# Scales of four token tiles at once, and squares of the mixer outputs summed on TensorE, in a hybrid attention and state-space layer

## The chip, the cores and the metric

One core of a Trainium2 chip runs the whole program. The metric is device time in microseconds (us), and lower is better. The kernel is written on a layer that takes tiles from pools, orders the instructions of each engine in a planner that simulates time, and then puts in the semaphore waits by itself. Each engine works through its own queue in that order.

## The reference

One decoder layer over 1024 tokens of width 1024. What matters here:

```python
mod = silu(c) @ ada_w + ada_b                    # sh1, sc1, g1, sh2, sc2, g2
h = modulate(rmsnorm(x, norm1_g), sh1, sc1)
p = h @ w_in                                     # q, k, v (512 each), u (512)
q = rmsnorm(q.reshape(L, 8, 64), q_norm_g)       # per token and head
k = rmsnorm(k.reshape(L, 8, 64), k_norm_g)
o_attn = stick_breaking(q, k, v)                 # strictly causal, 8 heads
o_ssm = s5(u, ...)                               # 32 groups of 16 channels
o = concat(rmsnorm(o_attn, attn_out_g), rmsnorm(o_ssm, ssm_out_g))
x = x + g1 * (o @ w_out)
h = modulate(rmsnorm(x, norm2_g), sh2, sc2)
x = x + g2 * ((gelu(gate) * val) @ ffn_w_down)   # val, gate: causal conv of h @ ffn_w_up
```

## The kernel before, in words

The program is one straight sequence without loops at run time. Its stages in the profiled execution are: norm and projection of u (0 to 95 us); projections of q, k and v, with the four batches of the state-space part and most of the modulation vectors among them (95 to 342 us); attention over eight heads, with the output projection of the state-space half as filler (342 to 580 us); the output projection of the attention half and the second norm (565 to 660 us); the gated MLP (to the end).

The middle stage is what the change touches first. Two loops (L592 to L625) run over q and k (cix) and over pairs of token tiles (tq). For each of the two tiles j of a pair, `proj` (L549) makes 24 products into a PSUM tile (tag "mm", three of them); ScalarE copies it to the SBUF tile `qk` (L603) and squares it in place (L605); VectorE sums the squares by head into `qssq` (L606). Then, once for a pair, VectorE forms 1/sqrt in 12 small operations on 16 columns (L607, and `rsqrt`, L71 to L80: a shift, a seed, three Newton rounds of three operations). Then both tiles are scaled (L611), transposed on TensorE (L615), split into a high and a low part `hl` (L618 to L622), and written to DRAM (L624).

In front of every projection stands `ada_step(3)` (L601): three steps of a generator (`ada_back`, L560) that makes the modulation vectors g1, sh2 and sc2. For each of six blocks `ix` it takes one tile `ada_acc` [128, 512], clears it on GpSimd, and then eight times loads a tile `ada_raw` of 256 KB through SyncE's DMA queue (L568) and adds it, times one column, to `ada_acc` on VectorE (L569, recorded as L67). At the end of a block TensorE sums over partitions (`adps`, L573 or L577). `ada_acc`, `ada_raw` and the tile `uF` of `u_evac` (L197) share one tag "uF" with three buffers in the pool `wp`. While a block runs, `ada_acc` holds one of the three, so two are left for `ada_raw`. What is left of the generator after the last projection of v runs at L649. 48 loads and 48 VectorE operations are made in all.

Then the pools `psA`, `stg`, `wp` and `hp` are released (L653 to L656), and the attention's pools `op_`, `wo`, `osp`, `psZ`, `psT`, `psM`, `ap_` take their memory (L657 to L662). All pools are made with `reuse_waits="tile"` (L58).

`mix_scale` (L750) gives the scale of the norm of the mixer outputs. For each token tile ScalarE squares four slices of 128 channels into `osq` (L755; one buffer), VectorE adds the four slices into `otot` (L757), and one product with a column of ones sums over partitions into a column of `nps` (L758). It runs for eight token tiles of the state-space half early in the attention (`ssm_stats`, L789), and for eight tiles of the attention half in the last head (`tail_stats`, L837).

Of the kernel before, what the change touches and what calls it, by code (L numbers as in the profile page):

```python
# [9 lines left out]
F32 = mybir.dt.float32  # L10
# [3 lines left out]
AF = mybir.ActivationFunctionType  # L14
ALU = mybir.AluOpType
AX = mybir.AxisListType
# [19 lines left out]
def hybrid_layer_kernel(  # L36
# [17 lines left out]
    act, dve, pool, pe, sp = nc.scalar, nc.vector, nc.gpsimd, nc.tensor, nc.sync  # L54
# [5 lines left out]
    def tt(eng, out, a, b, op):  # L60
        eng.tensor_tensor(out=out, in0=a, in1=b, op=op)  # L61
# [7 lines left out]
    MUL, ADD, SUB = ALU.mult, ALU.add, ALU.subtract  # L69

    def rsqrt(pl, dst, v, n):  # L71

        i = pl.tile([128, n], I32, tag="rs_i", name="rs_i")
        h = pl.tile([128, n], F32, tag="rs_h", name="rs_h")
        dve.tensor_scalar(out=i, in0=v.bitcast(I32), scalar1=1, scalar2=None, op0=ALU.logical_shift_right)
        ts(dve, dst.bitcast(I32), i, -1.0, RSQRT_SEED, MUL, ADD)
        for _ in range(3):
            stt(h, dst, -0.5, dst, MUL, MUL)
            tt(dve, h, h, v, MUL)
            stt(dst, h, 1.5, dst, ADD, MUL)  # L80
# [3 lines left out]
    small = alloc("small", bufs=2)  # L84
# [13 lines left out]
    ones = const.tile([128, 128], F32, name="ones")  # L98
# [34 lines left out]
    wp = alloc("w_in")  # L133
# [60 lines left out]
            pe.matmul(o, lhsT=ll, rhs=rh, start=False, stop=(k == 7))  # L194

    def u_evac(m, hf):
        uF = wp.tile([128, 8, 64], F32, tag="uF", name="uF", bufs=3)  # L197
        act.activation(out=uF, in_=u_ps[m, hf].rearrange("p (c j) -> p j c", j=8), func=AF.Copy)
        sp.dma_start(out=u_d[m * 128:(m + 1) * 128, :, hf * 64:(hf + 1) * 64], in_=uF)

# [348 lines left out]
    def proj(cix, t, his, los):  # L549
        o = psA.tile([128, 512], F32, tag="mm", name="qkvp", bufs=3)  # L550
        for k in range(NK):
            lh, ll = hhi[k][:, t * 128:(t + 1) * 128], hlo[k][:, t * 128:(t + 1) * 128]
            pe.matmul(o, lhsT=lh, rhs=his[k], start=(k == 0), stop=False)  # L553
            pe.matmul(o, lhsT=lh, rhs=los[k], start=False, stop=False)  # L554
            pe.matmul(o, lhsT=ll, rhs=his[k], start=False, stop=(k == NK - 1))  # L555
        return o
# [3 lines left out]
    def ada_back(ix):  # L560

        kind, o = divmod(ix * 512, 1024)
        acc = wp.tile([128, 512], F32, tag="uF", name="ada_acc", bufs=3)
        pool.memset(acc, 0.0)
        sp.dma_start(out=acc[0:1, :], in_=ada_br[ix:ix + 1, :])
        for r in range(8):
            raw = wp.tile([128, 512], F32, tag="uF", name="ada_raw", bufs=3)
            sp.dma_start(out=raw, in_=ada_r[ix, :, r])  # L568
            stt(acc, raw, c_sb[:, r:r + 1], acc, MUL, ADD)  # L569
            yield  # L570
        ps = psA.tile([128, 512], F32, tag="aux", name="adps")
        if kind == 0:
            pe.matmul(ps, lhsT=ones, rhs=acc, start=True, stop=True)  # L573
            act.activation(out=g1row[:, o:o + 512], in_=ps, func=AF.Copy)
        else:
            for j in range(4):
                pe.matmul(ps[:, j:j + 1], lhsT=acc[:, j * 128:(j + 1) * 128], rhs=ones[:, 0:1], start=True, stop=True)  # L577
            ks = slice(o // 128, o // 128 + 4)
            if kind == 1:
                act.activation(out=S2c[:, ks], in_=ps[:, 0:4], func=AF.Copy)  # L580
            else:
                stt(A2[:, ks], ps[:, 0:4], 1.0, n2g_sb[:, ks], ADD, MUL)
        yield
# [7 lines left out]
    ssm_at = {(0, 0): 0, (0, 1): 1, (0, 3): 2, (1, 1): 3}  # L591
    for cix in range(2):  # L592
        his, los = load_wchunk(cix)
        for tq in range(4):
            if (cix, tq) in ssm_at:
                ssm_batch(ssm_at[cix, tq])
            qk = stg.tile([128, 2, 8, 64], F32, tag="qk", name="qk", bufs=2)
            ssq = small.tile([128, 2, 8], F32, tag="qssq", name="qssq")
            inv = small.tile([128, 2, 8], F32, tag="qinv", name="qinv")
            for j in range(2):  # L600
                ada_step(3)  # L601
                o = proj(cix, tq * 2 + j, his, los)
                act.activation(out=qk[:, j].rearrange("p h d -> p (h d)"), in_=o, func=AF.Copy)  # L603
                ov = o.rearrange("p (h d) -> p h d", d=64)
                act.activation(out=o, in_=o, func=AF.Square)  # L605
                dve.tensor_reduce(out=ssq[:, j, :], in_=ov, op=ADD, axis=AX.X)  # L606
            ts(dve, ssq, ssq, 1.0 / HD, EPS, MUL, ADD)  # L607
            rsqrt(small, inv.rearrange("p a b -> p (a b)"), ssq.rearrange("p a b -> p (a b)"), 16)
            for j in range(2):
                t = tq * 2 + j  # L610
                tt(dve, qk[:, j], qk[:, j], inv[:, j, :].unsqueeze(2).to_broadcast([128, 8, 64]), MUL)  # L611
                tp = psA.tile([128, 512], F32, tag="qt", name="qkT", bufs=1)
                qf = qk[:, j].rearrange("p h d -> p (h d)")
                for a_ in range(4):
                    pe.transpose(tp[:, a_ * 128:(a_ + 1) * 128], qf[:, a_ * 128:(a_ + 1) * 128], ident)  # L615
                hl = stg.tile([128, 2, 512], F32R, tag="hl", name="hl", bufs=2)
                if cix == 0:
                    act.activation(out=hl[:, 0], in_=tp, func=AF.Copy, scale=gqk)  # L618
                    stt(hl[:, 1], tp, gqk, hl[:, 0].bitcast(F32), MUL, SUB)
                else:  # L620
                    act_copy(hl[:, 0], tp)
                    tt(dve, hl[:, 1], tp, hl[:, 0].bitcast(F32), SUB)  # L622
                for r in range(2):
                    act.dma_start(out=qk_d[cix, r].rearrange("(a p) t -> p a t", p=128)[:, :, t * 128:(t + 1) * 128],  # L624
                                 in_=hl[:, r].bitcast(F32).rearrange("p (a t) -> p a t", t=128))  # L625
# [124 lines left out]
    def mix_scale(pl, ps, src, ts_, jc, inv):  # L750

        for c, t in enumerate(ts_):
            s_, v = mix_view(src, t, jc)
            sq = pl.tile([128, 4, 128], F32, tag="osq", name="osq", bufs=1)
            act.activation(out=v(sq), in_=s_, func=AF.Square)  # L755
            tot = pl.tile([128, 128], F32, tag="otot", name="otot", bufs=1)
            dve.tensor_reduce(out=tot, in_=sq.rearrange("p k c -> p c k"), op=ADD, axis=AX.X)  # L757
            pe.matmul(ps[:, c:c + 1], lhsT=tot, rhs=ones[:, 0:1], start=True, stop=True)  # L758
            yield
        n = len(ts_)  # L760
        ssq = small.tile([128, n], F32, tag="ossq", name="ossq")
        ts(dve, ssq, ps[:, 0:n], 1.0 / 512.0, EPS, MUL, ADD)
        rsqrt(small, inv, ssq, n)
# [506 lines left out]
```

## Time and profile before

| | us |
|---|---|
| median of 3 runs | 1331.42 (1327.92 to 1335.95) |
| profiled execution | 1326.97 |
| its span | 1324.6 |
| PE busy | 1213.3 (92%) |
| DVE busy | 1010.3 (76%) |
| ACT busy | 587.1 (44%) |
| POOL busy | 467.5 (35%) |

The span runs from the first to the last instruction of the profiled execution; 2.4 us lie around it. PE is TensorE, DVE VectorE, ACT ScalarE, POOL GpSimd, SP SyncE; SPq is the queue through which SyncE issues transfers. A busy share over the whole span is a mean over stages with different limits, so the stages are read one by one.

### The profile page before, as it was taken

Reading aid. Unit: us, or ns where it says so; the run is one execution under the profiler, and the core shown is the slowest. Engines: PE = TensorE matmul, PEld = TensorE weight load, DVE = VectorE, ACT = ScalarE, POOL = GpSimd, SP = SyncE. Lnnn points to the kernel's source line nnn. Section 1 sums busy time; section 2 is a strip of 40 time slices with the busy share of each in tenths; the row PEclk is TensorE's granted clock in tenths of the full one; section 3 lists DMA queues with packets and bytes.
Section 4 is the critical chain, followed back from the end, with each engine's and each line's share of the span. In section 5 each row is a group of like instructions: output and inputs, shape, how many; then the busy total and the mean of one; then the engine's idle time right before and its main releaser. Section 6 shows DMA issues by size and latency. Waiting matters only on the chain.

```text
span 1324.6 us, 16659 instructions
## 1 busy us (share of the span) xinstructions
PE 1213.3 (92%) x5752; PEld 992.6 (75%) x5752; DVE 1010.3 (76%) x1543; ACT 587.1 (44%) x1003; POOL 467.5 (35%) x367
## 2 busy tenths in 40 slices
PE   5879899989678989679999998999999999999998
PEld 4767778767566777567777876788888888888887
DVE  6999997983788898988898878878887773345334
ACT  5431233331475677546654534454545453223220
POOL 4462443430563344930035544345554510000000
PEclk9898889999778999789999999999999999999999
DMA  8462455558943666115022233222222165447442
GB/s 342 163 144 50 117 139 152 143 140 231 265 105 96 204 188 203 42 56 170 30 88 103 81 104 104 96 96 72 96 72 96 49 203 186 143 160 253 148 138 104
DMA packets 125631, 177.83 MB, mean 134 GB/s; under 512 B 36454, under 2 KB 73958, under 8 KB 124524
## 3 DMA queue, kind: packets, MB, share of 16 engines
q1 hardware_dynamic: 105484, 156.85, 38.0%
q10 hardware_dynamic: 20064, 19.93, 4.5%
q8 instruction: 45, 0.74, 0.2%
q14 instruction: 38, 0.31, 0.1%
HBM read 134.67 MB, written 40.89 MB: 133 GB/s over the span
## 4 chain that ended last, share of the span: by engine, by line
PE 58%; DVE 25%; DMA 7%; issue 5%; ACT 3%; POOL 2%; SPq 1%; DVEq 0%; ACTq 0%; POOLq 0%
PE dnps L1181 6%; PE dnps L1180 6%; PE dnps L1182 6%; PE up_a L986 5%; PE up_a L985 5%; PE up_a L987 5%; DVE ada_acc L67 3%; DMA ada_raw<-in_ada_r_dram 3%; DVE nb L703 3%; PE up_c L986 2%; PE up_c L987 2%; PE up_c L985 2%; PE wops L776 2%; DVE cv L67 2%; PE wops L778 2%
## 5 line engine op out<-in xcount | busy, mean ns | idle before, releaser
L67 DVE SCALAR_TENSOR_TENSOR cv<-up,cols_sb,cv 128x1023 f32<-128x1023 f32 (+1 forms) x88 | 136.6, 1554 | 16.6 <-ACT cv L1106 15.9
L61 POOL TENSOR_TENSOR S<-upraw 128x512 f32<-128x512 f32 x40 | 72.8, 1820 | 208.0 <-DMA upraw<-in_w_up_dram 144.7
L61 DVE TENSOR_TENSOR alo<-araw,ahi 128x1024 fp32r<-128x1024 f32 x44 | 53.9, 1224 | 120.2 <-ACT ahi L160 120.1
L1181 PE MATMUL dnps<-wdlo,ahi 128*128 128x512 f32 x352 | 136.9, 389 | 0.0
L1182 PE MATMUL dnps<-wdhi,alo 128*128 128x512 f32 x352 | 136.9, 389 | 0.0
L1180 PE MATMUL dnps<-wdhi,ahi 128*128 128x512 f32 x352 | 134.7, 389 | 0.0
L61 POOL TENSOR_TENSOR sig<-sig,nb 128x127 f32<-128x127 f32 (+3 forms) x64 | 93.2, 1464 | 84.4 <-DVE nb L703 53.7
L160 ACT ACTIVATE ahi<-araw 128x1024 fp32r<-128x1024 f32 x44 | 46.6, 1059 | 144.4 <-PE dnps L1181 127.3
L703 DVE TENSOR_TENSOR_SCAN nb<-nb 128x128 f32<-128x128 f32 (+3 forms) x64 | 108.6, 1710 | 1.5 <-ACT nb L701 1.2
L61 DVE TENSOR_TENSOR uplo<-S,uphi 128x512 fp32r<-128x512 f32 x80 | 90.7, 1140 | 19.8 <-ACT uphi L160 19.4
L67 DVE SCALAR_TENSOR_TENSOR ada_acc<-ada_raw,c_sb,ada_acc 128x256 f32<-128x256 f32 (+1 forms) x97 | 75.0, 787 | 24.9 <-DMA ada_raw<-in_ada_r_dram 23.0
L160 ACT ACTIVATE uphi<-S 128x512 fp32r<-128x512 f32 x80 | 49.1, 625 | 89.5 <-POOL S L61 69.4
L61 POOL TENSOR_TENSOR cv<-cv 128x1024 f32<-128x1024 f32 x22 | 53.9, 2451 | 98.3 <-ACT cv L1110 88.8
L553 PE MATMUL qkvp<-w_hi,hhi 128*128 128x512 f32 x192 | 78.3, 409 | 5.6 <-DVE qssq L606 2.9
L554 PE MATMUL qkvp<-w_lo,hhi 128*128 128x512 f32 x192 | 78.1, 407 | 0.8 <-POOL w_lo L61 0.8
L555 PE MATMUL qkvp<-w_hi,hlo 128*128 128x512 f32 x192 | 78.2, 407 | 0.0
L1180 PEld LDWEIGHTS dnps<-wdhi,ahi 128*128 128x128 f32 x352 | 66.1, 188 | 13.8
L1182 PEld LDWEIGHTS dnps<-wdhi,alo 128*128 128x128 f32 x352 | 66.1, 188 | 13.7
L1181 PEld LDWEIGHTS dnps<-wdlo,ahi 128*128 128x128 f32 x352 | 66.1, 188 | 13.6
L160 ACT ACTIVATE uphi<-upraw 128x512 fp32r<-128x512 f32 x68 | 41.7, 627 | 55.8 <-PE up_c L986 22.4
L710 PE MATMUL wT<-ident,sig 128*128 128x128 f32 x288 | 50.4, 302 | 14.1 <-POOL sig L61 8.7
L714 ACT ACTIVATE wh<-wT 128x512 fp32r<-128x512 f32 (+2 forms) x96 | 45.4, 497 | 37.6 <-PE wT L710 24.2
(328 smaller groups left out, 3479.5 us busy)
## 6 DMA issues: line engine op xcount, KB each, us to landing
upraw<-in_w_up_dram SPq DMA_DIRECT2D x88, 256.0 KB, 3.1
araw<-a_d SPq DMA_DIRECT2D x44, 512.0 KB, 3.5
ada_raw<-in_ada_r_dram SPq DMA_DIRECT2D x48, 256.0 KB, 3.0
a_d<-cv ACTq DMA_DIRECT2D x22, 512.0 KB, 2.6
wdraw<-in_w_down_dram SPq DMA_DIRECT2D x44, 256.0 KB, 3.6
ada_raw<-in_ada_a_dram SPq DMA_DIRECT2D x8, 1024.0 KB, 9.4
qk_d<-hl ACTq DMA_DIRECT2D x32, 256.0 KB, 2.9
q<-qk_d SPq DMA_DIRECT2D x32, 256.0 KB, 5.7
```

The costliest lines, as they stand in the source:

```text
L61: eng.tensor_tensor(out=out, in0=a, in1=b, op=op)
L67: dve.scalar_tensor_tensor(out=out, in0=a, scalar=s, in1=b, op0=op0, op1=op1)
L160: act.activation(out=o, in_=i, func=AF.Copy)
L553: pe.matmul(o, lhsT=lh, rhs=his[k], start=(k == 0), stop=False)
L555: pe.matmul(o, lhsT=ll, rhs=his[k], start=False, stop=(k == NK - 1))
L703: dve.tensor_tensor_scan(out=nb[:, 0:n][:, ::-1], data0=nb[:, 0:n][:, ::-1], data1=nb[:, 0:n][:, ::-1], initial=1.0, op0=MUL, op1=ALU.bypass)
L985: pe.matmul(ps, lhsT=hi[:, kt, :], rhs=rh, start=(first and kt == 0), stop=False, skip_group_check=True)
L986: pe.matmul(ps, lhsT=hi[:, kt, :], rhs=rl, start=False, stop=False, skip_group_check=True)
L987: pe.matmul(ps, lhsT=lo[:, kt, :], rhs=rh, start=False, stop=(kt == 3), skip_group_check=True)
L1180: pe.matmul(o[t], lhsT=hi[:, a], rhs=whi, start=(m == 0), stop=False)
L1181: pe.matmul(o[t], lhsT=hi[:, a], rhs=wlo, start=False, stop=False)
L1182: pe.matmul(o[t], lhsT=lo[:, a], rhs=whi, start=False, stop=(m == NM - 1))
```

## The change

Three things are done.

The loop over pairs becomes a loop over groups of four tiles: `qssq` and `inv` have 32 columns, the 12 small operations run once for four tiles, and scaling and transposes of four tiles follow. The tiles `qk` become single ones with five buffers (before: double ones with two). The batches of the state-space part keep their places between the projections.

The tag "uF" goes from three buffers to two, for `uF`, `ada_acc` and `ada_raw` alike.

In `mix_scale` the addition on VectorE and the tile `otot` are gone; four products, one for each slice of `osq`, accumulate in the column of `nps`. `osq` gets two buffers.

```diff
     def u_evac(m, hf):
-        uF = wp.tile([128, 8, 64], F32, tag="uF", name="uF", bufs=3)
+        uF = wp.tile([128, 8, 64], F32, tag="uF", name="uF", bufs=2)
...
-        acc = wp.tile([128, 512], F32, tag="uF", name="ada_acc", bufs=3)
+        acc = wp.tile([128, 512], F32, tag="uF", name="ada_acc", bufs=2)
...
-            raw = wp.tile([128, 512], F32, tag="uF", name="ada_raw", bufs=3)
+            raw = wp.tile([128, 512], F32, tag="uF", name="ada_raw", bufs=2)
...
-        for tq in range(4):
-            if (cix, tq) in ssm_at:
-                ssm_batch(ssm_at[cix, tq])
-            qk = stg.tile([128, 2, 8, 64], F32, tag="qk", name="qk", bufs=2)
-            ssq = small.tile([128, 2, 8], F32, tag="qssq", name="qssq")
-            inv = small.tile([128, 2, 8], F32, tag="qinv", name="qinv")
-            for j in range(2):
+        for tq in range(2):
+            qks = []
+            ssq = stg.tile([128, 4, 8], F32, tag="qssq", name="qssq")
+            inv = stg.tile([128, 4, 8], F32, tag="qinv", name="qinv")
+            for j in range(4):
+                if (cix, tq * 2 + j / 2) in ssm_at:
+                    ssm_batch(ssm_at[cix, tq * 2 + j // 2])
                 ada_step(3)
-                o = proj(cix, tq * 2 + j, his, los)
-                act.activation(out=qk[:, j].rearrange("p h d -> p (h d)"), in_=o, func=AF.Copy)
+                o = proj(cix, tq * 4 + j, his, los)
+                qk = stg.tile([128, 8, 64], F32, tag="qk", name="qk", bufs=5)
+                qks.append(qk)
+                act.activation(out=qk.rearrange("p h d -> p (h d)"), in_=o, func=AF.Copy)
...
-            rsqrt(small, inv.rearrange("p a b -> p (a b)"), ssq.rearrange("p a b -> p (a b)"), 16)
-            for j in range(2):
-                t = tq * 2 + j
-                tt(dve, qk[:, j], qk[:, j], inv[:, j, :].unsqueeze(2).to_broadcast([128, 8, 64]), MUL)
+            rsqrt(stg, inv.rearrange("p a b -> p (a b)"), ssq.rearrange("p a b -> p (a b)"), 32)
+            for j in range(4):
+                t = tq * 4 + j
+                tt(dve, qks[j], qks[j], inv[:, j, :].unsqueeze(2).to_broadcast([128, 8, 64]), MUL)
...
-            sq = pl.tile([128, 4, 128], F32, tag="osq", name="osq", bufs=1)
+            sq = pl.tile([128, 4, 128], F32, tag="osq", name="osq", bufs=2)
             act.activation(out=v(sq), in_=s_, func=AF.Square)
-            tot = pl.tile([128, 128], F32, tag="otot", name="otot", bufs=1)
-            dve.tensor_reduce(out=tot, in_=sq.rearrange("p k c -> p c k"), op=ADD, axis=AX.X)
-            pe.matmul(ps[:, c:c + 1], lhsT=tot, rhs=ones[:, 0:1], start=True, stop=True)
+            for kk in range(4):
+                pe.matmul(ps[:, c:c + 1], lhsT=sq[:, kk, :], rhs=ones[:, 0:1], start=(kk == 0), stop=(kk == 3))
```

## Rows read from the trace of the kernel before

**Rows 1.** Busy time by engine, with share of the span and instructions (page, part 1).

```profile
PE 1213.3 (92%) x5752; PEld 992.6 (75%) x5752; DVE 1010.3 (76%) x1543; ACT 587.1 (44%) x1003; POOL 467.5 (35%) x367
```

**Rows 2.** Busy time by stretch: stretch, length, engines (instructions), clock, DMA share, GB/s.

```profile
95.00:190.00 95.00, 82.78 (x425) 68.21 (x425) 91.36 (x197) 22.21 (x36) 33.89 (x30) 0.88 0.40 102
...
292.00:342.00 50.00, 43.43 (x210) 35.74 (x210) 19.53 (x29) 9.33 (x16) 3.98 (x8) 0.98 0.70 208
342.00:420.00 78.00, 59.04 (x286) 46.63 (x285) 69.23 (x82) 50.13 (x108) 48.84 (x44) 0.73 0.56 151
...
565.00:640.00 75.00, 66.52 (x321) 54.41 (x321) 61.54 (x167) 41.70 (x82) 9.41 (x10) 0.95 0.33 113
```

**Rows 3.** The chain that ended last, at 292 us: start, duration, what.

```profile
292.50 3.12 DMA ada_raw<-in_ada_r_dram
295.72 0.76 DVE ada_acc L67
296.50 3.66 DMA ada_raw<-in_ada_r_dram
```

**Rows 4.** Waits of SyncE's queue, 60 to 345 us: total us, times, longest.

```profile
SPq L568 <- DVE ada_acc L67: 53.1, 30, 6.2
```

**Rows 5.** Timeline of DVE: start, duration, line, operation, releaser of idle time before.

```profile
122.42 0.74 DVE L67 SCALAR_TENSOR_TENSOR ada_acc<-ada_raw,c_sb,ada_acc 128x512 f32<-128x512 f32 x1
...
139.23 0.75 DVE L67 SCALAR_TENSOR_TENSOR ada_acc<-ada_raw,c_sb,ada_acc 128x512 f32<-128x512 f32 x1
...
291.72 0.75 DVE L67 SCALAR_TENSOR_TENSOR ada_acc<-ada_raw,c_sb,ada_acc 128x512 f32<-128x512 f32 x1
...
338.83 0.75 DVE L67 SCALAR_TENSOR_TENSOR ada_acc<-ada_raw,c_sb,ada_acc 128x512 f32<-128x512 f32 x1 [2.11 <-DMA ada_raw<-in_ada_r_dram]
```

**Rows 6.** Timeline of PE where the projections end and attention begins.

```profile
335.47 0.39 PE L555 MATMUL qkvp<-w_hi,hlo 128*128 128x512 f32 x1
339.69 1.35 PE L577 MATMUL adps<-ones,ada_acc 128*128 128x1 f32 x8 [3.83 <-issue]
340.90 0.45 PE L697 MATMUL z<-k,q 128*128 128x128 f32 x1
```

**Rows 7.** The small DVE operations of L607 and L608, 95 to 345 us, by form.

```profile
L67 DVE SCALAR_TENSOR_TENSOR rs_h<-qinv 128x16 f32<-128x16 f32 x24 | 9.5, 402 | 0.2
...
L75 DVE TENSOR_SCALAR rs_i<-qssq 128x16 int32<-128x16 int32 x8 | 6.3, 787 | 0.0
...
L61 DVE TENSOR_TENSOR rs_h<-rs_h,qssq 128x16 f32<-128x16 f32 x24 | 5.7, 243 | 0.2
...
L67 DVE SCALAR_TENSOR_TENSOR qinv<-rs_h,qinv 128x16 f32<-128x16 f32 x24 | 5.0, 215 | 0.3
L64 DVE TENSOR_SCALAR qinv<-rs_i 128x16 int32<-128x16 int32 x8 | 4.3, 538 | 0.0
L64 DVE TENSOR_SCALAR qssq<-qssq 128x16 f32<-128x16 f32 x8 | 2.8, 350 | 0.1
```

**Rows 8.** The addition in `mix_scale`, products with one column, and PE's wait (360 to 420 us).

```profile
L757 DVE TENSOR_REDUCE otot<-osq x16: 994/1048/1092, 368.7 to 608.5; 128x128 f32<-128x512 f32 x16
...
11.17 6.96 PE L212 MATMUL mps<-c_sb,ada_raw 128*128 128x1 f32 x32 [11.17 <-DVE inv L67]
...
61.62 0.61 PE L220 MATMUL mps<-ones,ada_acc 128*128 128x1 f32 x4 [0.81 <-DVE ada_acc L67]
62.09 0.48 PE L193 MATMUL ups<-hlo,wu_hi 128*128 128x512 f32 x1
...
PE nps L758 <- DVE otot L757: 4.6, 5, 1.7
```

**Rows 9.** SyncE's queue, and the transposes that last read `sig`, at the attention's end.

```profile
580.20 1.76 SPq L1068 DMA_DIRECT2D g1row<-in_ada_br_dram  x4
...
609.02 7.89 SPq L904 DMA_DIRECT2D upraw<-in_w_up_dram  x6
...
L710 PE MATMUL wT<-ident,sig x288: 270/273/477, 344.3 to 573.0; 128*128 128x128 f32 x144
```

More of the change, by code (lines that the diff above doesn't have):

```diff
@@ L607, in hybrid_layer_kernel @@
             ts(dve, ssq, ssq, 1.0 / HD, EPS, MUL, ADD)
-            rsqrt(small, inv.rearrange("p a b -> p (a b)"), ssq.rearrange("p a b -> p (a b)"), 16)
-            for j in range(2):
-                t = tq * 2 + j
-                tt(dve, qk[:, j], qk[:, j], inv[:, j, :].unsqueeze(2).to_broadcast([128, 8, 64]), MUL)
+            rsqrt(stg, inv.rearrange("p a b -> p (a b)"), ssq.rearrange("p a b -> p (a b)"), 32)
+            for j in range(4):
+                t = tq * 4 + j
+                tt(dve, qks[j], qks[j], inv[:, j, :].unsqueeze(2).to_broadcast([128, 8, 64]), MUL)
                 tp = psA.tile([128, 512], F32, tag="qt", name="qkT", bufs=1)
-                qf = qk[:, j].rearrange("p h d -> p (h d)")
+                qf = qks[j].rearrange("p h d -> p (h d)")
                 for a_ in range(4):
```

## The prediction

> **What bounds the kernel now.** I read the busy shares first [rows 1]: TensorE is busy 92% of the span, so no single engine explains the rest, and the stages have to be read by themselves [rows 2]. From 95 to 190 us VectorE is busy 91.36 of 95 us and TensorE 82.78: both are nearly full. From 292 to 342 us the picture turns: VectorE is busy 19.53 of 50 us and TensorE 43.43, and neither is the limit at the end. The chain that ended last shows what is. At 292 us it goes from a load of `ada_raw` to the VectorE operation on it and on to the next load: 3.12 us, 0.76 us, 3.66 us [rows 3]. The reader is to see a chain through memory: the next load cannot start until the operation has freed its buffer. SyncE's queue says the same over the whole stage: it stood 53.1 us, in 30 waits, at L568 until `ada_acc` operations were done [rows 4]. The 48 operations run from 122.42 to 338.83 us [rows 5]. The last projection of v ends at about 335.8 us, TensorE then waits 3.83 us for the last `adps`, and the first score product of the attention starts at 340.90 us, behind it [rows 6]. So the chain of modulation loads is the last thing that ends before the attention, already with two buffers for `ada_raw`.
>
> **The change part by part. The two buffers of "uF".** With `ada_acc` holding one, a single one is left for `ada_raw`. Each step then is load, operation, load, one after the other. Such a step lasts from 291.72 [rows 5] to 295.72 [rows 3]: 4.00 us, of which 3.12 us are the load. With two buffers, where little else was going on, eight operations ran from 122.42 to 139.23 us [rows 5], 16.81 / 7 = 2.40 us a step. The price of a step without overlap is therefore at least 4.0 us. In the planner's order it may be as much as twice 2.40 = 4.8 us, since two steps in flight at 2.40 us mean 4.8 us for one buffer's round, and the order of VectorE and SyncE is fixed by that plan.
>
> I applied both to the 48 starts (the first and last are in [rows 5]; 47 intervals, sum 216.4 us). Intervals that are longer than the floor stay, since other transfers in SyncE's queue made them; 26 of the 47 lie under 4.0 us and are raised. With a floor of 4.0 us the sum is 260.6 us, so the last operation starts at 383.1 us; with 4.8 us it is 406.4 us. Both assume that the planned pace holds to the end. Where the projections are over (at 330 us, say), nothing competes any more: with the floor of 4.0 us, 12 steps are left then, and these, bare, with some 2 us more at each change of block, end at 376 us; with the floor of 4.8 us 15 are left, and the end is 390 us. Against 338.8 us the chain is thus 38 to 68 us later; I take 48 us, near the two bare ends (mean 44) and a little above, since SyncE's transfers for the state-space part, each of which the chain must get past, will stand in its way more often with one buffer.
>
> The Trainium skill has a rule that speaks against this edit: "Trainium Kernel Development and Optimization", section Best Practices, asks for double buffering so that transfers overlap with compute. The trace agrees where the two buffers did overlap: 2.40 us a step against 4.00 us. By that rule alone, without the wait of the attention, the edit would cost 48 times the difference of 1.6 us.
>
> Does the attention wait for this chain? Its data does not: g1 is needed first, and its two blocks are early; sh2 and sc2 are needed after the attention. But the attention's pools take the memory of `wp` and `psA`, in which `ada_acc`, `ada_raw` and `adps` lie. How the planner treats this can be seen at the attention's end [rows 9]. `upraw`, a load that needs nothing but memory that `ap_` gave back, is first issued at 609.02 us, although `sig`, which lay there as I work out the layout, was last read at 573.0 us; at 580.20 us the same queue had time for a load that belongs far later in the program. It came right behind the last tile of `ap_`, `otot` at 608.5 us [rows 8]. So the planner places a new pool's tiles behind the last tile of the old pool. If it does so here, every instruction of the attention is queued behind the chain's last operations on every engine, TensorE's score products behind `adps` as now [rows 6], and TensorE idles: 48 us are added in full.
>
> **u_evac with two buffers.** The third evacuation waits for a write of u. Cost 0 to 3 us on ScalarE and TensorE; VectorE's preparation of the state-space part, which ends later, covers it. I take 0.
>
> **Four tiles at a time.** The small operations take 9.5 + 6.3 + 5.7 + 5.0 + 4.3 + 2.8 = 33.6 us for 96 of them [rows 7]; 48 remain, so 16.8 us of VectorE are gone in a stage where it is 91.36 of 95 us busy at first [rows 2]. 32 columns in place of 16 cost little: a duration far over the least one comes from waiting, not from columns. What the saving is worth: nothing where TensorE is the limit next (it is at 82.78 of 95 us), up to 12 us if all slack of TensorE in that stretch were taken up. If the chain decides the end, it only brings the planned positions of the remaining operations forward, by perhaps 2 us; I take 2. Against it stands that after the last tile of k four tiles instead of two are still to be transposed while v already comes; three PSUM tiles of the next projections can be filled meanwhile, and these cover it; if they did not, TensorE would stand for one to a few of VectorE's operations, which is within A's range.
>
> **mix_scale.** 16 additions of 1.048 us leave VectorE, 16.8 us [rows 8]. TensorE gets three more products for each tile, each in two passes: 16 x 6 = 96 passes. Four passes in a row took 62.09 - 61.62 = 0.47 us, 0.117 us each; 32 took 6.96 us in the kernel's first products, 0.217 us each [rows 8]. So TensorE gets 11 to 21 us. For the eight tiles from 367 us on the clock was 0.73 of full and VectorE busy 69.23 of 78 us, TensorE 59.04 [rows 2]: here VectorE's 8.4 us are worth most, and PE's 4.6 us of waiting for `otot` [rows 8] go with them; the 48 passes cost at most 10.4 us on an engine with 19 us free. For the eight in the last head TensorE is busy 66.52 of 75 us, and 48 passes cost 5.6 us at the quick rate; there gain and cost cancel. I take 2 us gain in all, between -6 and +6.
>
> The sum: 1327.0 + 48 - 2 - 2 = 1371 us, against the profiled execution of 1326.97, which lies 4.5 us under the median of the runs.
>
> **The rivals.** A: as above, the attention stands behind the chain. Its own range: at the low end 38 us, less all 12 us of the four-tile scale and 6 us of the mixer, 1347 us; at the high end 68 us and 6 us lost at the mixer, 1401 us.
> B, the other sign: the planner lets the attention pass the chain, since the waits that it writes are by tile. Then the late operations, some 15 at 0.75 us, run among the attention's, and VectorE has 16.8 us less to do beside the projections, besides those 15 operations. The projections' stage is then shortened to what TensorE leaves: 95 to 342 us by 5 to 12 us, the mixer gives its 2. For it speaks that memory is handed on by tile (L58) and that no data of the attention comes from the chain; against it speak the 609.02 us of `upraw`. It decides from the point where the first score product stands ahead of the last `adps`. 1327 - 8 - 2 = 1317 us (1308 to 1324).
> C: the attention passes the chain in the plan, but the queues of SyncE and VectorE stop at each late load. The chain gets a load of 3.1 us for each of 15 steps, of which a part stalls VectorE, busy 69.23 of 78 us there: with a third of the load, an estimate, 15 x 1 us takes back what B gains, and 5 us more: 1332 us (1324 with half of it, 1345 with twice).
> The change does what it says in each of these; that the four-tile scale changes nothing is part of A.
>
> **How the numbers follow.** A 0.62, B 0.24, C 0.14. The forecast is A's, 1371 us. The range has to hold eight in ten: A's 1347 to 1401 holds 0.55, C 0.13, and B is taken in from 1314 us, another 0.16: 1314 to 1401, with 0.84. A alone: 1347 to 1401. About 0.5%, 6.6 us, is what a measurement of this kernel can tell from no change. Faster by more: most of B, 0.21. Within: C's middle and B's upper edge, 0.13. Slower: A and the rest of C, 0.66.
>
> **What would show it.** In the new profile: loads of `ada_raw` one at a time, 4 us and more apart; `adps` of the last block at 370 to 410 us; a gap on TensorE of 30 us or more between the last product of v (325 to 335 us) and the first score product, right behind `adps`; from there to the end the old duration within 5 us. The small operations: 48 in place of 96. `nps` with 128 passes and no PE wait on `otot`. Wrong would be the forecast if score products stand before the last `adps`, or if the planner starts the chain much earlier than now and most of its 48 steps are done by 330 us.

## The result, and the profile after

| | before | after |
|---|---|---|
| median of the runs | 1330.34 us (4 runs, 1327.92 to 1335.95) | 1374.22 us (4 runs, 1370.72 to 1377.6) |
| span of the profiled execution | 1324.6 us | 1368.9 us |
| mean granted clock of TensorE | 0.952 | 0.941 |

The changed kernel takes 1.0333 times as long, with a 95% interval of 1.0308 to 1.0358. The forecast was 1371 us. One execution of e1 (4119.42 us, the one that was profiled) and one of the kernel before (1705.23 us) were disturbed and are left out of every ratio below; without its own, e1's median is 1384.05 us instead of 1385.53.

The busy times are read first, beside [rows 1]; this is part 1 of the page of the kernel after:

```profile
PE 1213.7 (89%) x5848; PEld 997.7 (73%) x5848; DVE 990.4 (72%) x1479; ACT 585.8 (43%) x1003; POOL 474.6 (35%) x367
```

VectorE has 64 instructions and 19.9 us less to do, TensorE 96 instructions more and the same busy time, and yet the span has grown by 44.3 us. No engine has so much more work, so most of the time is waiting. Where it lies, the table by stretch of the kernel after shows (columns as in [rows 2]):

```profile
95.00:190.00 95.00, 85.00 (x450) 68.39 (x451) 85.02 (x175) 25.73 (x42) 38.48 (x35) 0.90 0.35 86
...
292.00:342.00 50.00, 41.29 (x196) 33.28 (x196) 22.95 (x39) 10.26 (x15) 3.13 (x4) 0.90 0.70 196
342.00:420.00 78.00, 23.95 (x118) 20.81 (x119) 30.30 (x34) 21.22 (x40) 21.23 (x18) 0.56 0.39 123
```

From 342 to 420 us every engine is mostly idle: TensorE is busy 23.95 of 78 us, where it was 59.04 [rows 2]. The timeline of TensorE in the kernel after, beside [rows 6], gives the hole its edges (start, duration, line, operation, in brackets the idle time before it and what ended it):

```profile
338.00 0.39 PE L555 MATMUL qkvp<-w_hi,hlo 128*128 128x512 f32 x1
363.60 1.87 PE L577 MATMUL adps<-ones,ada_acc 128*128 128x1 f32 x8 [25.20 <-DVE ada_acc L67]
395.61 1.86 PE L577 MATMUL adps<-ones,ada_acc 128*128 128x1 f32 x8 [30.15 <-DVE ada_acc L67]
397.33 0.45 PE L699 MATMUL z<-k,q 128*128 128x128 f32 x1
```

The last product of v is 2.5 us later than before, and then TensorE waits 25.20 and 30.15 us for two `adps`; right behind the last one stands the first score product, 56.4 us later than before. The chain that ended last, of the kernel after, shows what `adps` waited for:

```profile
348.82 10.16 DMA ada_raw<-in_ada_r_dram
...
368.30 0.76 DVE ada_acc L67
369.08 2.65 DMA ada_raw<-in_ada_r_dram
371.82 0.76 DVE ada_acc L67
372.60 2.92 DMA ada_raw<-in_ada_r_dram
...
395.61 1.88 PE adps L577 x8
```

One load, one operation, one load: nothing overlaps. A bare step lasts 371.82 - 368.30 = 3.5 us, and one load that was issued behind five loads of queries and keys (256 KB each) and the one of `oS` (2048 KB) took 10.16 us.

### The profile page after: what moved, and what is told of

Its sections match the earlier page's. It is cut to its first block, busy times and chain, and to the rows that moved or that the text cites. A ratio compares the mean times of both kernels' runs of the same rounds, so it can differ in the third digit from the quotient of the medians.

```text
span 1368.9 us, 16818 instructions
## 1 busy us (share of the span) xinstructions
PE 1213.7 (89%) x5848; PEld 997.7 (73%) x5848; DVE 990.4 (72%) x1479; ACT 585.8 (43%) x1003; POOL 474.6 (35%) x367
## 4 chain that ended last, share of the span: by engine, by line
PE 55%; DVE 23%; DMA 11%; issue 4%; POOL 4%; ACT 2%; SPq 0%; DVEq 0%; ACTq 0%; POOLq 0%
PE dnps L1182 6%; PE dnps L1181 6%; PE dnps L1183 6%; DMA ada_raw<-in_ada_r_dram 6%; PE up_a L987 5%; PE up_a L986 5%; PE up_a L988 5%; DVE ada_acc L67 3%; DVE nb L705 3%; PE up_c L987 2%; PE up_c L988 2%; PE up_c L986 2%; DVE cv L67 2%; DVE wl L61 1%; PE wops L777 1%
## 5 line engine op out<-in xcount | busy, mean ns | idle before, releaser
L67 DVE SCALAR_TENSOR_TENSOR ada_acc<-ada_raw,c_sb,ada_acc 128x256 f32<-128x256 f32 (+1 forms) x97 | 67.8, 713 | 90.4 <-DMA ada_raw<-in_ada_r_dram 90.4
L61 POOL TENSOR_TENSOR sig<-sig,nb 128x127 f32<-128x127 f32 (+3 forms) x64 | 97.0, 1525 | 90.8 <-DVE nb L705 71.7
L703 ACT ACTIVATE nb<-z 128x512 f32<-128x512 f32 (+2 forms) x96 | 48.1, 501 | 48.3 <-PE z L702 38.6
L61 DVE TENSOR_TENSOR uplo<-upraw,uphi 128x512 fp32r<-128x512 f32 x68 | 61.6, 919 | 5.6 <-ACT uphi L160 5.6
```

Source lines behind the costliest of these rows:

```text
L67: dve.scalar_tensor_tensor(out=out, in0=a, scalar=s, in1=b, op0=op0, op1=op1)
```

## The experiments

Their times, as ratios to the kernel before run on the same chip; "start" is the first score product, and "to up" the time from there to the first evacuation of `up_a`, the first one behind the attention. Both are from the profiled execution (before: 340.9 and 298.3 us). The runs were made on three chips: the kernel before had a median of 1330.80 us beside e1 to e4, 1329.24 beside e5 to e8 and 1327.51 beside e9 to e12. Runs of different groups are therefore compared by their ratios.

| run | what differs from before | median us | ratio (95%) | start | to up |
|---|---|---|---|---|---|
| after | all three parts | 1374.22 | 1.0333 (1.0308 to 1.0358) | 397.3 | 283.9 |
| e1 | two buffers | 1385.53 | 1.0414 (1.0386 to 1.0443) | | |
| e5 | two buffers | 1382.76 | 1.0404 (1.0371 to 1.0436) | 411.4 | 286.5 |
| e6 | two buffers, scales | 1379.38 | 1.0377 (1.0351 to 1.0404) | 400.4 | 290.4 |
| e2 | scales | 1334.58 | 1.0039 (1.0023 to 1.0055) | 352.1 | 293.3 |
| e3 | mixer | 1324.45 | 0.9958 (0.9939 to 0.9977) | 340.3 | 298.0 |
| e4 | scales, mixer | 1336.70 | 1.0046 (1.0028 to 1.0064) | 348.9 | 299.2 |
| e7 | all three, late blocks moved | 1350.49 | 1.0152 (1.0126 to 1.0179) | 342.9 | 318.5 |
| e8 | scales of the queries alone | 1341.56 | 1.0081 (1.0052 to 1.0109) | 352.0 | 298.3 |
| e9 | mixer, four buffers | 1317.17 | 0.9916 (0.9891 to 0.9941) | 334.4 | 296.8 |
| e10 | scales, mixer, three products more | 1334.74 | 1.0060 (1.0039 to 1.0081) | 347.4 | 295.5 |
| e11 | mixer, chain asked for earlier | 1330.83 | 1.0021 (1.0001 to 1.0041) | 347.4 | 300.9 |
| e12 | as e10, four buffers of "uF" and of `qk` | 1332.03 | 1.0026 (1.0009 to 1.0043) | 344.6 | 293.9 |

**Two buffers alone (e1, e5).** The kernel before with one edit, at each of the three places with the tag:

```
-        uF = wp.tile([128, 8, 64], F32, tag="uF", name="uF", bufs=3)
+        uF = wp.tile([128, 8, 64], F32, tag="uF", name="uF", bufs=2)
```

> The kernel before with only the buffers of "uF" set from 3 to 2; the small operations and the mixer's squares stay as they were. Theory A (the modulation chain without overlap holds the attention, and nothing else of the change costs anything): the last adps stands 45 to 60 us later than its 338.8 us of before, the first score product right behind it, and the time is 1370 to 1388 us. The upper end holds if nothing of the delay is given back in the attention, the lower if the same 12 us come back there as in the changed kernel, because work was done during the wait. Rival R1 (the regrouping into four tiles pushed the chain back, the buffer count alone is harmless): 1328 to 1340 us.

> The kernel before with only the buffers of "uF" set from 3 to 2, once more, to see where its 1385 us go. From the first score product to the first evacuation of `up_a` the kernel before takes 298.3 us and the changed one 283.9. Theory R3 (the wait ahead of the attention lets the other engines and the queues do work that is then missing from the attention): some 284 to 288 us here, and the first score product at 405 to 412 us. Theory R4 (the shorter attention is due to the two other parts of the change): 295 to 300 us here, and the first score product at 393 to 398 us.

Measured: 1385.53 us, and 1382.76 us in the second run, whose profile is read here. R1 is out: without any regrouping the delay is there, and larger. A's time holds, its 45 to 60 us do not: the last `adps` is 70.0 us later. From the timeline of TensorE in e5:

```profile
337.83 0.39 PE L555 MATMUL qkvp<-w_hi,hlo 128*128 128x512 f32 x1
...
409.72 1.84 PE L577 MATMUL adps<-ones,ada_acc 128*128 128x1 f32 x8 [29.92 <-DVE ada_acc L67]
411.42 0.45 PE L697 MATMUL z<-k,q 128*128 128x128 f32 x1
```

The start is 70.5 us late, but the attention is 298.3 - 286.5 = 11.8 us shorter. Both numbers are R3's, and R4 is out. (The runs without the wait, e7 apart, lie between 293.3 and 300.9 us, so some us of the 11.8 may be the scatter of single profiles.) R3 had said that the queues do work during the wait that is then missing from the attention. In the chain of before the stretch from 341 to 386 us was led by the load of `vsb` (18.4%), GpSimd's work on `sig` (13.5%) and the write of v (12.9%); in e5 the first 45 us of the attention have VectorE busy 43.83 us, where it was 38.03, at a DMA share of 0.29 instead of 0.76. The stretches of e5 and of the kernel before:

```profile
411.00:456.00 45.00, 35.14 (x161) 28.45 (x162) 43.83 (x48) 30.14 (x64) 36.28 (x26) 0.68 0.29 82
```

```profile
341.00:386.00 45.00, 34.20 (x160) 26.09 (x159) 38.03 (x39) 28.51 (x62) 33.98 (x25) 0.71 0.76 211
```

**Two buffers and the scales (e6).** The changed kernel with the mixer's sum on VectorE put back:

```
-            sq = pl.tile([128, 4, 128], F32, tag="osq", name="osq", bufs=2)
+            sq = pl.tile([128, 4, 128], F32, tag="osq", name="osq", bufs=1)
...
-            for kk in range(4):
-                pe.matmul(ps[:, c:c + 1], lhsT=sq[:, kk, :], rhs=ones[:, 0:1], start=(kk == 0), stop=(kk == 3))
+            tot = pl.tile([128, 128], F32, tag="otot", name="otot", bufs=1)
+            dve.tensor_reduce(out=tot, in_=sq.rearrange("p k c -> p c k"), op=ADD, axis=AX.X)
+            pe.matmul(ps[:, c:c + 1], lhsT=tot, rhs=ones[:, 0:1], start=True, stop=True)
```

> The changed kernel with the mixer's squares summed on VectorE again (two buffers of "uF" and the scales of four tiles stay). If the mixer's gain of some 5 us adds up with the rest: 1378 to 1382 us. R3: the wait has already freed VectorE, the mixer brings little, 1373 to 1377 us. Against the run with two buffers alone (1385.5 us) the difference is the regrouping's under the wait: by the run of the regrouping alone it would be 5 us slower, 1390; by the saving of 16 us on VectorE, if it lets the chain end earlier, 1376 to 1382 us.

Measured: 1379.38 us, start at 400.4 us; inside 1378 to 1382 us, so the gains add up, and R3's 1373 to 1377 is out. Under the wait the regrouping brings the start forward by 11.0 us, from 411.4, and gives 3.9 back behind it. In time it is worth 0.37% (4.9 us) against e1 and 0.27% (3.6 us) against e5; both lie inside the interval of such a difference, some 0.4%, so that it gains in time is likely and not shown. The mixer's products are worth another 0.44% or 5.9 us, a little more than theirs.

**The late blocks out of the way (e7).** The changed kernel, with blocks 2 to 5 of the modulation in four tiles of `us`, which lies beside the attention's pools, and made between the attention's tiles instead of ahead of them:

```
-    ada_gen = (q for ix in range(6) for q in ada_back(ix))
+    ada_gen = (q for ix in range(2) for q in ada_back(ix))
...
+    late_gen = (q for ix in range(2, 6) for q in ada_back(
+        ix, lambda nm: us.tile([128, 512], F32, tag="S", name=nm, bufs=4), lambda: psB_new("adps")))
...
+            if hd < 6:
+                with tc.issue_after(here[0].ins):
+                    next(late_gen, None)
...
```

> The changed kernel, two buffers of "uF" kept, but the four later blocks of the modulation (sh2 and sc2, 32 of the 48 steps) taken through four tiles of a pool that lies beside the attention, in steps between its tiles; their products go to the mixer's PSUM tiles. The work is the same. Theory A (the pools' hand-over holds the attention): the first score product starts at 325 to 345 us, right behind the last product of v, and the time is 1320 to 1345 us, the upper part if the 24 us of VectorE cost as much in the attention as they free ahead of it. Rival R5 (the attention is late because the loads themselves are late, whoever holds the memory): above 1360 us.

Measured: 1350.49 us, 23.7 under the changed kernel. The same loads and operations are there, the last of the 48 at 440.6 us, long behind the first score product, which starts at 342.9 us. R5 is out: loads that are later still do not hold the attention when they are neither ahead of it in the program nor in memory that it takes. From the timeline of TensorE in e7:

```profile
336.69 0.39 PE L555 MATMUL qkvp<-w_hi,hlo 128*128 128x512 f32 x1
342.93 0.47 PE L702 MATMUL z<-k,q 128*128 128x128 f32 x1 [5.85 <-DVE vt L61]
```

What ends the wait now is `vt`, the last evacuation of v, although a score product reads only q and k. What `vt` does for it is to empty the PSUM tile of the last product of v, so this wait fits a hand-over of memory, tile by tile.

e7 changes two things at once, the memory of the late blocks and their place in the program. The trace of the kernel before speaks against the place in the program as the cause. There, too, work that waits is passed by work that the program has later: the last state-space batch stands ahead of the third tile of k in the program, and on TensorE its last products came behind 419 of the 576 products of the projections, among those of v (q and k have 384):

```profile
291.56 0.38 PE L516 MATMUL yps<-S,W 64*128 64x128 f32 x2
```

A place in the program alone would thus not have kept the score products behind 55 idle us. That the planner's rule for new pools did it is the reading that is left; no run changes the memory alone.

The time missed its expectation by 5 us. From the start to `up_a` e7 takes 318.5 - 283.9 = 34.6 us more than the changed kernel and 20.2 more than before: the head start of the wait is gone, and 32 operations, 24 us of VectorE, with their loads now stand in the attention.

**The scales alone (e2), the mixer alone (e3), and both (e4).** e2 and e4 are the changed kernel with the three buffers put back, e2 also with the mixer's sum on VectorE; e3 is the kernel before with the mixer's products.

> The kernel before with only the regrouping of the scales of queries and keys into four tiles; "uF" keeps its 3 buffers and the mixer's squares are summed on VectorE as before. Theory A: 16 us less of small operations on VectorE, the chain's end between 325 and 345 us, and a time of 1318 to 1331 us, 2 us less taken as likeliest. R1: the chain ends 30 us and more later here too, and the time is 1355 to 1380 us.

> The kernel before with only the squares of the mixer summed by four accumulating products; "uF" and the scales stay. Nothing before the attention differs, so the first score product should start at 340 to 342 us. Theory A as predicted: -6 to +6 us, so 1324 to 1336 us, likeliest 1328. Rival R2 (the 12 us that the changed kernel gained after the attention's start are the mixer's, since VectorE is the limit there): 1316 to 1321 us. Rival R3 (those 12 us are work done during the wait before the attention): within 2 us of the kernel before.

> The changed kernel whole, with the 3 buffers of "uF" put back. Theory A: the modulation chain overlaps again, the first score product starts at 330 to 345 us, and the time is the sum of the two other parts, 1314 to 1328 us, some 50 us under the changed kernel. R1: the time stays above 1350 us.

Measured: 1334.58, 1324.45 and 1336.70 us. The mixer alone gains 0.42%, 5.6 us: inside what A allowed, below R2's, above R3's. It shows in the medians; the two profiled executions (spans 1324.5 and 1324.6 us) differ too little to show its place. R2 and R3 are both out as they stand here, but R3's mechanism is the one that e5 shows: of the 12 to 14 us that the attention got shorter, e5 has 11.8 without the mixer. e4 confirms that the two buffers are the loss (37.5 us between it and the changed kernel, 55 us in e1 without the regrouping), but both e2 and e4 miss: the regrouping costs 0.39%, 5.2 us, where a gain was expected, and the mixer brings nothing on top of it. The chain isn't the reason: its last operation starts at 338.2 us in e2, as before. The whole stage of TensorE up to the first score product, in the kernel before and in e2 (stretch, length, busy time and instructions, granted clock, DMA share, GB/s):

```profile
95.00:340.90 245.90, 221.82 (x1157) 0.92 0.52 142
```

```profile
95.00:352.10 257.10, 232.50 (x1157) 0.86 0.50 139
```

The same 1157 instructions, the same idle time (24.1 and 24.6 us), but 10.7 us more of busy time at a lower clock. (The two profiled executions lie 9.4 us apart and the medians 5.2, so the pair shows where the time goes more than how much it is.) One place has a large share. In e2 and in the kernel before, the same stretches:

```profile
262.00:281.00 19.00, 16.31 (x74) 1.00 0.81 197
281.00:302.00 21.00, 20.32 (x72) 0.52 0.29 88
```

```profile
262.00:281.00 19.00, 15.28 (x64) 0.91 0.70 175
281.00:302.00 21.00, 20.92 (x122) 1.00 0.47 132
```

In e2 the granted clock is 0.52, nearly the lower of its two levels, for 21 us in which TensorE is busy 20.32; it issues 72 instructions there, the kernel before 122. A pair of `yps` products (L514) takes 0.79 us there (at 291.56 us) and 0.49 in the kernel before (at 290.81 us). (1 - 0.52) x 21 = 10 us is the most that it can have cost. It begins behind this wait of TensorE in e2:

```profile
281.69 0.58 PE L516 MATMUL yps<-S,W 64*128 64x128 f32 x2 [2.19 <-DVE S L61]
```

**Queries alone in groups of four (e8).** From e2:

```
-        for tq in range(2):
+        gn = 4 if cix == 0 else 2
+        for tq in range(8 // gn):
```

> The regrouping alone, with 3 buffers of "uF", but four tiles at once for the queries only; the keys go in pairs as before. Theory T1 (the 4 us that the regrouping costs come from the keys' last group: four tiles are transposed and split while v already comes, behind loads of the chain in VectorE's queue): 1326 to 1331 us. Theory T2 (they come from TensorE's half clock from 282 to 302 us, behind its 2.2 us of waiting for the last state-space batch, which the regrouping brings about by shifting VectorE's order): only if that stretch is gone, too, does the time fall; with it 1333 to 1337 us.

Measured: 1341.56 us, slower than e2. T1 is out: the keys' last group of four isn't what costs. From 280 to 300 us the clock of e8 is 0.61, so T2's condition is met; its time is 4.6 us above what T2 allowed, and TensorE also waits 28.1 us in all up to the start, 4.0 more than before, 6.6 of them for one `vt`.

**Products that cover the wait (e10, e12).** The changed kernel with three buffers, and

```
+        if ft == 3:
+            dm = psA.tile([128, 512], F32, tag="aux", name="dmy")
+            for _ in range(3):
+                pe.matmul(dm, lhsT=ident, rhs=S[0].rearrange("p q c -> p (q c)"), start=True, stop=True)
```

> The changed kernel with 3 buffers of "uF" (1336.7 us) and three products more on TensorE whose result nobody reads: 128x128 by 128x512 on the last state-space batch's S, placed just ahead of the products that waited 2.2 us at 281.7 us. Nothing else is changed. Theory T2 (what the regrouping costs is TensorE's half clock behind that wait: 0.50 of full from 285 to 295 us, 0.80 to 305): the granted clock stays at 1.0 there, the first score product starts 6 to 10 us earlier, at 339 to 343 us, and the time is 1326 to 1331 us, though TensorE has some 2.5 us more to do. Rival T3 (the clock is a by-product, VectorE's order sets the pace): the start stays at 348 to 352 us and the time at 1335 to 1340 us.

> As the run with the three covering products, but with a fourth buffer of "uF" and four in place of five for `qk`, so that the next group's first tile waits for the last one's. If T2 and A both hold, 1320 to 1328 us; if `qk` with four buffers holds up the next group, TensorE waits there and the time is 1330 us and more.

Measured in e10: 1334.74 us and a start at 347.4. Its ratio of 1.0060 would be 1338.8 us on the chip for which the ranges were set, which is T3's range and no better than e4. The products ran from 273.4 to 276.2 us and the wait shrank from 2.2 to 0.9 us, but the clock fell all the same, a little later and for a shorter time, as the stretches of TensorE in e10 show:

```profile
275.00:285.00 10.00, 9.07 (x41) 0.79 0.18 58
285.00:295.00 10.00, 10.00 (x37) 0.53 0.48 149
295.00:305.00 10.00, 10.00 (x55) 1.00 0.46 132
```

So the experiment doesn't tell T2 from T3: the wait was not taken away. e12 measured 1332.03 us (1334.3 by its ratio), in the range of its second case, but not for the reason given there, since TensorE waits no longer than without the regrouping. Its clock is 1.00 from 285 to 335 us, and its start at 344.6 us is still late, so the stretch behind the last batch is not all of it. Its pair is e9, with four buffers and without the regrouping; here the stretches up to the start of e12 and of e9:

```profile
95.00:344.60 249.60, 226.70 (x1162) 0.91 0.50 143
```

```profile
95.00:334.40 239.40, 215.86 (x1157) 0.94 0.53 149
```

Again the idle time is alike (22.9 and 23.5 us) and the busy time is 10.8 us longer, 4.3 us of them the three products (280.32 to 284.59 us). In three pairs of profiles (e2 and before, e4 with 229.88 us busy and before, e12 and e9) the attention thus starts later with the regrouping because TensorE is busy longer with the same work, at a lower granted clock, and not because it waits longer. e8 is the exception, with 7.1 us more busy and 4.0 us more waiting. Over whole executions the mean granted clock is a weak guide: in e8 the one with 0.955 took 1330.62 us and the five with 0.940 to 0.946 took 1340.65 to 1342.55, but one of e2 with 0.899 took 1333.76, no more than the others. What lets the clock fall in one order of the instructions and not in the other is open.

**A fourth buffer (e9), and the chain asked for earlier (e11).** Both are the kernel before with the mixer's products; e9 has `bufs=4` at the three places with the tag "uF", e11 `ada_step(4)` in place of `ada_step(3)`.

> The kernel before with the mixer's products and a fourth buffer of "uF", the opposite of the change's edit; the scales stay. Theory A (the chain's overlap sets when the attention starts, as long as it ends last): the chain ends well before the last product of v, the first score product starts 2 to 6 us earlier than with three buffers (340.3 us), and the time is 1318 to 1324 us, against 1324.5 with three. Rival R6 (three buffers were already enough; what is left ahead of the attention is the projections'): 1322 to 1327 us, the start unchanged within 1 us.

> The kernel before with the mixer's products, and four steps of the modulation chain asked for ahead of each projection in place of three; three buffers of "uF". It shifts the chain earlier in the program's order without changing its step. Theory A: the end of the chain falls below the last product of v if the planner follows, the first score product at 336 to 339 us, the time 1318 to 1324 us. R6: no change to 1324.5 within 3 us. A third outcome is possible, that the chain's operations ahead of the projections take VectorE, 91 of 95 us busy there, and the projections end later: 1326 to 1332 us.

Measured in e9: 1317.17 us, the fastest of all, 0.84% under the kernel before. The chain ends at 305.0 us:

```profile
305.00 0.75 DVE L67 SCALAR_TENSOR_TENSOR ada_acc<-ada_raw,c_sb,ada_acc 128x512 f32<-128x512 f32 x1 [0.54 <-DMA ada_raw<-in_ada_r_dram]
```

and the attention starts 5.9 us earlier than in e3. R6 is out by the start. In time the gain over e3 is 0.42%; the ratio of 0.9916 on the chip for which the ranges were set is 1319.6 us, inside A's and under R6's. In e11 the chain ends early as well, at 317.7 us, yet the start is at 347.4 us: the last product of v is at 345.6 us instead of 334.1, and among TensorE's waits is one of 8.17 us for a `vt`. VectorE's and TensorE's timelines of e11 show why:

```profile
309.23 0.75 DVE L67 SCALAR_TENSOR_TENSOR ada_acc<-ada_raw,c_sb,ada_acc 128x512 f32<-128x512 f32 x1 [2.10 <-DMA ada_raw<-in_ada_r_dram]
...
312.77 1.92 DVE L67 SCALAR_TENSOR_TENSOR ada_acc<-ada_raw,c_sb,ada_acc 128x512 f32<-128x512 f32 x1 [0.93 <-DMA ada_raw<-in_ada_r_dram]
314.62 1.28 DVE L61 TENSOR_TENSOR vt<-qkvp,vt 128x512 fp32r<-128x512 f32 x2
```

```profile
315.35 0.79 PE L553 MATMUL qkvp<-w_hi,hhi 128*128 128x512 f32 x1 [8.17 <-DVE vt L61]
```

The evacuation stands in VectorE's queue behind operations that wait for their loads; 2.10 + 0.93 = 3.0 of the 8.17 us are VectorE's idle time for them. Of the 7.1 us by which e11 starts later than e3, 3.2 are more idle time of TensorE and 3.9 more busy time, at 0.89 instead of 0.92 of the clock. The time of 1330.83 us is the third outcome's (1333.6 by its ratio, a little above it): with the same buffers, more steps ahead of the projections make these end later.

## Why the prediction was right, point by point

**That the attention waits for the chain** was the step that decided, and it held: the last `adps` at 395.6 us lies in the 370 to 410 named, the first score product follows it, and e7 and e9 move the start by moving the chain. `upraw` [rows 9] stands beside the last tile of `ap_` in the new profile too, first issued at 649.32 us with the last `nps` at 649.5. It does not prove the planner's rule, though, since in both kernels it also comes right behind four writes of `xs`, which the program has ahead of it. SyncE's queue in the kernel before ends them at 588.71 + 20.20 = 608.91 us, and the kernel after shows the same:

```profile
588.71 20.20 SPq L852 DMA_DIRECT2D x_d<-xs  x4
```

```profile
629.55 19.64 SPq L853 DMA_DIRECT2D x_d<-xs  x4
649.32 2.17 SPq L905 DMA_DIRECT2D upraw<-in_w_up_dram  x4
```

The rule thus rests on e7, on the wait for `vt` there, and on the order of `yps` in the kernel before. "Every instruction of the attention is queued behind" was too strong: two squares into `osq` and two copies into `ohi` (from 358.36 us), six of GpSimd's memsets (from 364.11 us) and the loads of q, k and `oS` passed during the wait. That they are the 11.8 us of e5 fits, and is not measured apart. B and C were wrong as to the place of the wait, though C's mechanism exists: in e11 late loads stop VectorE's queue and TensorE with it. C's upper value was added up wrongly: 1317 + 30 is 1347 us, not 1345.

**The chain's length.** 48 us were taken; it ended 56.0 us later, in 38 to 68, and 70.0 us in e5. Behind 330 us 14 operations were left (12 to 15 predicted), and a bare step is 3.5 to 3.8 us (the last one 4.7), not 4.0. Two things were mis-sized. Loads of queries, keys and `oS` got ahead of the chain's, and the four steps from 343.9 to 368.3 us took 24.4. And the change of block, put at 2 us, is where the second buffer is lost: `ada_acc` of the next block takes one, the old `ada_acc` keeps the other until TensorE gets to its `adps`. The first time this lasted 54 us, the four other times 5.5 to 6.6. From VectorE's timeline of the kernel after:

```profile
146.38 0.75 DVE L67 SCALAR_TENSOR_TENSOR ada_acc<-ada_raw,c_sb,ada_acc 128x512 f32<-128x512 f32 x1 [1.08 <-DMA ada_raw<-in_ada_r_dram]
...
200.43 0.73 DVE L67 SCALAR_TENSOR_TENSOR ada_acc<-ada_raw,c_sb,ada_acc 128x512 f32<-128x512 f32 x1
...
394.81 0.75 DVE L67 SCALAR_TENSOR_TENSOR ada_acc<-ada_raw,c_sb,ada_acc 128x512 f32<-128x512 f32 x1 [3.96 <-DMA ada_raw<-in_ada_r_dram]
```

and between the first two, on TensorE and in SyncE's queue:

```profile
188.71 1.02 PE L573 MATMUL adps<-ada_acc,ones 128*128 128x512 f32 x2
```

```profile
190.41 0.39 SPq L568 DMA_DIRECT2D ada_raw<-in_ada_r_dram  x1
```

The load is issued right behind the product. In the kernel before the same hold was there, one buffer milder. The two buffers for `ada_raw` that the text ahead of the prediction counts are two only while no older `ada_acc` waits for its product, and the first block's `adps` came as late as

```profile
201.33 1.92 PE L573 MATMUL adps<-ada_acc,ones 128*128 128x512 f32 x2
```

so the second block had one, with eight operations from 143.62 to 195.41 us, 7.4 us a step (VectorE is nearly full there, too [rows 2]).

So 48 us came near 56 partly by luck. The prediction made its delay from many steps, each raised to 4.0 us, 33 us of them behind the ninth operation. Measured, the ninth operation is already 56.8 us late (200.43 instead of 143.62 us), and from it to the last it takes 194.4 us, where before it took 195.2: some steps are longer, others shorter, and the sum is nothing.

**From the start to the end.** "Within 5 us of the old duration" failed: from the first score product to the end it is 971.6 us, where it was 983.7. Its first part, up to `up_a`, is 14.4 us shorter, of which e5 has 11.8 from the wait alone. So it is luck that the forecast fits to 3 us (and the profiled execution, 1370.72 us, still closer): two misses cancel, the start 10 us later than taken (56.4 against 48 - 2), the rest 10 us shorter than the 2 us of the mixer. 56.4 - 14.4 + 2.3 (behind `up_a`) are the span's 44.3 us.

**The scales.** 48 small operations take 17.1 us, 16.5 less (16.8 predicted); the largest group of the kernel after:

```profile
L67 DVE SCALAR_TENSOR_TENSOR qinv<-rs_h,qinv 128x32 f32<-128x32 f32 x12 | 5.0, 417 | 0.3
```

One takes 417 ns, where it was 215 with half the columns [rows 7]; over all six the mean rises only from 350 to 356 ns, so 32 columns cost little, as taken. Their worth is a term with the wrong sign where the chain isn't the limit: 2 us of gain were taken, 0 to 12 allowed, and e2 lost 5.2. The bound "nothing, where TensorE is next" left out that another order can slow TensorE itself. In the change it brings the start forward by 11.0 us, as the wait for the chain is what it shortens, and 4 to 5 us of that are left in the time, inside the interval.

**The mixer.** 128 passes, and no wait of TensorE for `otot`; 5.6 us gained alone and 5.9 in the change, inside the -6 to +6, above the 2 taken. Why it was more than 2, the profiles do not show, and on top of the regrouping (e4 against e2) it was nothing.

**u_evac.** ScalarE's waits for the writes of u grew from 2.8 to 7.3 us and the last evacuation moved from 92.72 to 96.06 us, with the first projection at 103.6 us instead of 103.4: 0, as taken.

**The rule of the Trainium skill** ("Trainium Kernel Development and Optimization", section Best Practices, on double-buffering) is borne out by e5 and e9: the step without overlap is 3.5 us and more, the start moves by 70.5 us one way and 5.9 the other with one buffer less or more. By the rule alone the prediction had 48 times 1.6, 77 us of chain; 56 were measured, and most of them came from one stop, not from 48 steps.

## What to carry to other kernels

A chain of loads that nobody needs soon can still hold a whole stage, if the next stage's pools take its memory: look at what was last in the old pool, not only at who reads the data. (e7 fits this; it moved the chain's place in the program along with its memory.) Count the buffers of a shared tag by who holds them, the accumulator of the old block and of the new one included, before one is taken away; here one more was worth 0.4% and one less cost 4%. Work that is taken from an engine off the path may be worth nothing or less than nothing when TensorE does the order that is left at a lower granted clock, as here at 0.86 instead of 0.92.

## What was not expected of the hardware

TensorE's granted clock stayed near its lower level (0.52 of full) for 21 us in which TensorE was busy 20.32 us, behind one wait of 2.19 us; in the kernel before, with 3.7 us of idle time in the 19 us ahead of the same place instead of 2.7, it stayed at 1.00. The idle time alone doesn't say what the clock did next. And a load of 256 KB, 2.7 us in the median, took 10.16 us behind five loads of queries and keys and the 2048 KB of `oS`, which itself took 10.2.
